# A hybrid mLSTM, convolution and expert layer on one core: TensorE sums the squares of the input piece by piece, in a kernel whose first stage is reordered by token halves

## The chip, the core and the metric

The kernel runs on one core of a Trainium2 chip. A core has five engines that run programs of their own and wait for one another by semaphores: TensorE (PE in the rows; its weight loads are shown apart as PEld), VectorE (DVE), ScalarE (ACT), GpSimd (POOL) and SyncE (SP), which here only issues DMA transfers. The metric is the device time of one execution in microseconds; lower is better. The time before is the median of three runs.

## The reference

One layer over 1024 latent tokens with a context of 256 tokens, width 1024, in float32. What matters here is how it begins:

```python
hx = _modulate(_rms_norm(x, g_pre_mix[l]), mx[0], mx[1])     # x * rsqrt(mean(x^2) + eps) * g * (1+scale) + shift
hc = _modulate(_rms_norm(ctx, g_pre_mix[l]), mc[0], mc[1])
yx, yc = _token_mixer(hx, hc, w_in[l], ...)                  # input projection, mLSTM, convolution, output projection
...
x = x + mx[5] * _rms_norm(_moe_ffn(hx, ...), g_post_ffn[l])  # 64 experts, top 8, and a shared one
```

`mx[0]` and `mx[1]` (shift and scale) are columns of `silu(c) @ w_ada + b_ada`. The norm needs, for each token, the sum of the squares of its 1024 features. After the projection there follow two scans of the mLSTM, a depthwise convolution of width 31, the output projection, the routing and the experts.

## The kernel before

`front` (L106) holds the input transposed: `X` has 8 pieces, each 128 features by 1024 tokens, loaded by eight transfers on SP's queue (L144). The stage works as follows.

- **Sums of squares** (`squares`, L147). For each piece k ScalarE writes the squares to a buffer (L151), and VectorE adds them to the sum in `vf`, the first 1024 columns of `va` (L153). So `vf` holds at the end 128 partial sums for each token.
- **Sum over partitions** (`sums`, L211). For each group of 128 tokens one matmul has the 128x128 block of `vf` as its weights and one column of ones as its moving operand (L213). VectorE scales the result (L214), and GpSimd raises it to the power of -0.5 (L215). It is done for groups 0 to 3, and then for groups 4 to 7.
- **Spread** (`spread`, L217). Four matmuls (L219) copy the four groups' factors to all 128 partitions, into half of the tile `rs`, which has 1024 columns in PSUM.
- **Scale and shift columns** (`products` and `shifts`). `products(k)` loads 1 MB of `w_ada` to a buffer `wa` and multiplies it by `silu(c)` (L183); ScalarE copies the result (L189), TensorE turns it (L192), and VectorE makes the columns `sh` and `gs` (L193, L194).
- **Modulation** (`modulate`, L222), for each piece k and each half j of 512 tokens: VectorE multiplies `X` by `gs` and `rs` (L224), ScalarE makes the rounded part `hH` (L225), VectorE the remainder `hL` (L226).
- **Projection** (`mm3`, L434). Two blocks of columns of the input weights (f = 8 and 4), each for two halves of the tokens, are accumulated over k in four PSUM tiles `pf`. Each step has three matmuls of 512 columns: `hH` by `wfH` (L436), `hL` by `wfH` (L437), `hH` by `wfL` (L438). Their weights are split in two parts by ScalarE (`wfH`, L50) and VectorE (`wfL`, L51).
- Before the first sums, six matmuls at L241 multiply pieces 3 to 5 of `X` by ones. Their results, in `rs`, are not used.

The program is written with a scheduler that keeps each engine's instructions in an order of priority; `with self.behind(...)` gives what stands in it the priority just behind the last instruction that was issued on that engine. Each engine then runs its instructions strictly in the order that came out. A float32 matmul shows in the trace as two records of TensorE, each with a weight load of its own: the four matmuls of L213 are eight records. Matmuls on the rounded parts (L436 to L438) are one record each.

What follows this stage is the rest of the projection, in which the convolution of the first blocks (`conv`, L419 on) runs on VectorE beside it, then the scans and the rest.

Of the kernel before, what the change touches and what calls it, by code (L numbers as in the profile page):

```python
# [32 lines left out]
class Layer:  # L33
# [72 lines left out]
    def front(self, cp):  # L106
# [40 lines left out]
        def squares(src, a, b):  # L147

            for k in range(8):
                sq = vf[:, NT * (1 + k % 3):][:, :b - a] if k else vf[:, a:b]  # L150
                nc.scalar.activation(sq, src[:, k], AF.Square)  # L151
                if k:
                    nc.vector.tensor_tensor(vf[:, a:b], vf[:, a:b], sq, op=OP.add)  # L153
# [10 lines left out]
        cs = small.tile([128, 8, 16, 2], F32, name="cs")  # L164
        nc.vector.tensor_copy(cs, csil.unsqueeze(2).to_broadcast([128, 8, 16, 2]))
        cs = cs.rearrange("p k r s -> p k (r s)")
        squares(X, 0, NX)
        with self.behind(mybir.EngineType.DVE):
            nc.vector.tensor_scalar(ba1[:, 8:], ba1[:, 8:], 1.0, None, op0=OP.add)
        pj, pj_ = self.pool("pj", 1, PSUM)  # L170
# [27 lines left out]
        def weights(t, pool=wf):  # L198
            if t not in wts:
                wr = wf.tile([128, 8, 128], F32, name="wfr", bufs=2)  # L200
                nc.sync.dma_start(wr, A["wf"][t])
                wH = pool.tile([128, 8, 128], F32R, name="wfH", bufs=2)
                wL = pool.tile([128, 8, 128], F32R, name="wfL", bufs=2)
                self.split(wH, wL, wr, nc.gpsimd if len(wts) > 1 else None)
                wts[t] = (wH, wL)
            return wts[t]

        ss = turned[:, :16]
        rs = pp.tile([128, NX], F32, name="rs")

        def sums(ss, a, b):  # L211
            for j in range(a, b):
                mm(ss[:, j - a:j - a + 1], vf[:, j * 128:j * 128 + 128], self.ones[:, :1], start=True, stop=True)  # L213
            nc.vector.tensor_scalar(rc[:, a:b], ss[:, :b - a], 1.0 / D, EPS, op0=OP.mult, op1=OP.add)  # L214
            nc.gpsimd.tensor_tensor(rc[:, a:b], rc[:, a:b], self.mhalf[:, a:b], op=OP.pow)  # L215

        def spread(rs, a, b):  # L217
            for j in range(a, b):
                mm(rs[:, (j - a) * 128:(j - a) * 128 + 128], rc[:, j:j + 1].to_broadcast([128, 128]), self.ident,  # L219
                   start=True, stop=True)  # L220
# [14 lines left out]

        U, Y = X[:, :4], X[:, 4:]
        first = [(f, j, pj.tile([128, 512], F32, name="pf", bufs=4)) for j in range(2) for f in (8, 4)]

        for k in range(3, 6):
            for j in range(2):  # L240
                mm(rs[:, :512], self.ones, X[:, k, 512 * j:512 * j + 512], start=True, stop=True)  # L241
        sums(ss, 0, 4)
        with self.behind():
            products(0)
        with self.behind():
            sums(ss[:, 4:], 4, 8)
        weights(8, small)
        with self.behind():
            spread(rs, 0, 4)
            shifts(0)  # L250
        with self.behind(mybir.EngineType.Activation):
            weights(4, small)
        with self.behind():
            spread(rs[:, 512:], 4, 8)
        for k in range(8):
            if k == 4:
                weights(9)
                weights(5)
            if k < 7:
                products(k + 1)  # L260
                shifts(k + 1)
            for j in range(2):
                s = slice(512 * j, 512 * j + 512)
                modulate(X[:, k, s], rs[:, s], hH[:, k, s], hL[:, k, s], k, 0)
            for f, j, ps in first:
                s = slice(512 * j, 512 * j + 512)
                self.mm3(ps, wts[f][0][:, k], wts[f][1][:, k], hH[:, k, s], hL[:, k, s], k == 0, k == 7)
        with tc.issue_after(self.wa1):
            for t, n in ((bf, "bf"), (cw, "convw"), (cv, "convv"), (ng, "normg")):
                nc.sync.dma_start(t, A[n])  # L270
# [1540 lines left out]
```

## Time and profile before

| What | Value |
|---|---|
| median of three runs | 1495.1 us (1492.36 to 1497.14) |
| the profiled execution | 1497.91 us, span 1496.1 us |
| TensorE busy | 1426.1 us, 95% of the span |
| VectorE busy | 1133.3 us, 76% |
| ScalarE busy | 753.7 us, 50% |
| GpSimd busy | 477.9 us, 32% |
| mean granted clock of TensorE | 0.986 |
| DMA | 371.64 MB, mean 248 GB/s |

The page divides the span into 40 slices of 37.4 us; TensorE is busy for 0.6 of the first one and for nearly all of the others. The stage that is changed lies in the first two slices. Times in rows are microseconds from the start of the span.

### The profile page before, as it was taken

To read this page: it belongs to the slowest core of one execution; us is meant where nothing else is said; L and a number is where in the kernel's file an instruction comes from. 1 tells how busy PE (TensorE), PEld (TensorE's weight loads), DVE (VectorE), ACT (ScalarE), POOL (GpSimd) and SP (SyncE) were. 2 spreads that over 40 slices of the span, in tenths; PEclk is the share of its full clock that TensorE was granted. 3 is DMA by queue.
4 is the path that set the end of the run, shared out by engine and by line. 5 is a ranking of instruction groups with operands and counts; after the bars stand their busy time and mean duration, and the time that the engine had idled before them with its cause. 6 is when DMAs were issued, how large, how long until landed. Compare 5 with 4: busy or idle time off the path is not lost. (4 is left out here: it accounts for less than half of the span.)

```text
span 1496.1 us, 22962 instructions
## 1 busy us (share of the span) xinstructions
PE 1426.1 (95%) x8211; PEld 1088.5 (73%) x8211; DVE 1133.3 (76%) x1942; ACT 753.7 (50%) x1241; POOL 477.9 (32%) x306
## 2 busy tenths in 40 slices
PE   6999999989999989999999999999999999999975
PEld 4688997765567755876788888888777777777764
DVE  5899979767867886744678788888777877777636
ACT  4421011245433344644566666776676767666621
POOL 1245001112213422233333333333334344455324
PEclk9999999999999999999999999999999999999998
DMA  8421051018653567997999999999999999999975
GB/s 314 176 71 43 1 189 40 19 48 287 221 187 115 193 240 275 357 294 246 306 288 327 331 322 319 333 343 339 316 342 299 321 342 310 315 352 318 337 251 209
DMA packets 94385, 371.64 MB, mean 248 GB/s; under 512 B 18269, under 2 KB 26789, under 8 KB 67770
## 3 DMA queue, kind: packets, MB, share of 16 engines
q1 hardware_dynamic: 65946, 298.48, 53.3%
q0 software_dynamic: 26032, 70.19, 19.2%
q10 hardware_dynamic: 2288, 1.45, 0.4%
q8 instruction: 66, 1.08, 0.3%
q14 instruction: 53, 0.43, 0.1%
HBM read 322.38 MB, written 62.19 MB: 257 GB/s over the span
## 5 line engine op out<-in xcount | busy, mean ns | idle before, releaser
L51 DVE TENSOR_TENSOR u<-u,u 128x1024 fp32r<-128x1024 f32 x354 | 422.0, 1220 | 124.7 <-ACT u L50 94.8
L50 ACT CAST u<-u 128x1024 fp32r<-128x1024 f32 x354 | 361.3, 1052 | 108.5 <-PE pgu L438 41.6
L1559 POOL DMA_INDIRECT acc<-yb,dst x98 | 194.4, 1983 | 351.7 <-ACT hTH L50 118.3
L436 PE MATMUL pgu<-u,xH 128*128 128x512 f32 x608 | 245.8, 404 | 0.4
L437 PE MATMUL pgu<-u,xH 128*128 128x512 f32 x608 | 238.8, 393 | 0.0
L438 PE MATMUL pgu<-u,xL 128*128 128x512 f32 x608 | 238.1, 392 | 0.0
L1439 POOL DMA_INDIRECT xg<-hxd,tok x98 | 123.6, 1261 | 194.1 <-DVE rwj L1347 68.6
L431 DVE SCALAR_TENSOR_TENSOR X<-X,cw 128x912 f32<-128x912 f32 (+14 forms) x120 | 152.0, 1291 | 1.1
L436 PEld LDWEIGHTS pgu<-u,xH 128*128 128x128 f32 x608 | 114.5, 188 | 25.5 <-ACT u L50 2.6
L438 PEld LDWEIGHTS pgu<-u,xL 128*128 128x128 f32 x608 | 114.3, 188 | 24.6
L437 PEld LDWEIGHTS pgu<-u,xH 128*128 128x128 f32 x608 | 114.5, 188 | 21.5
L436 PE MATMUL py<-u,hTH 128*128 128x512 f32 x304 | 122.1, 402 | 0.5 <-ACT hTH L50 0.5
L437 PE MATMUL py<-u,hTH 128*128 128x512 f32 x304 | 119.8, 394 | 0.0
L438 PE MATMUL py<-u,hTL 128*128 128x512 f32 x304 | 118.6, 395 | 0.0
L436 PE MATMUL pf<-hH,wfH 128*128 128x512 f32 x256 | 103.6, 408 | 0.0
L437 PE MATMUL pf<-hL,wfH 128*128 128x512 f32 x256 | 102.7, 401 | 0.7 <-DVE hL L226 0.6
L51 DVE TENSOR_TENSOR xL<-px,xH 128x512 fp32r<-128x512 f32 x152 | 97.5, 681 | 7.7 <-ACT xH L50 7.3
L438 PE MATMUL pf<-hH,wfL 128*128 128x512 f32 x256 | 102.3, 400 | 0.0
L50 ACT CAST xH<-px 128x512 fp32r<-128x512 f32 x152 | 83.9, 592 | 13.7 <-PE pgu L437 7.8
L1551 DVE COPY yb<-py 128x512 f32<-128x512 f32 x75 | 51.5, 687 | 46.3 <-PE py L438 45.8
L51 POOL TENSOR_TENSOR wfL<-wfr,wfH 128x1024 fp32r<-128x1024 f32 x14 | 48.0, 3428 | 118.2 <-ACT wfH L50 104.2
L1461 PE MATMUL px<-ident,xg 128*128 128x128 f32 x600 | 83.8, 274 | 1.1 <-DVE nl L1244 1.1
(431 smaller groups left out, 2515.6 us busy)
## 6 DMA issues: line engine op xcount, KB each, us to landing
u<-in_we_dram SPq DMA_DIRECT2D x192, 1024.0 KB
wa<-in_wa_dram SPq DMA_DIRECT2D x64, 256.0 KB
wa<-in_wa_dram SPq DMA_DIRECT2D x8, 1024.0 KB
wfr<-in_wf_dram SPq DMA_DIRECT2D x16, 512.0 KB
v<-acc SPq DMA_DIRECT2D x16, 512.0 KB
acc<-zero SPq DMA_DIRECT2D x13, 512.0 KB
u<-in_ws_dram SPq DMA_DIRECT2D x6, 1024.0 KB
X<-in_xT_dram SPq DMA_DIRECT2D x8, 512.0 KB
```

The costliest lines, as they stand in the source:

```text
L50: self.nc.scalar.copy(H, src)
L51: return (eng or self.nc.vector).tensor_tensor(L, src, H.bitcast(F32), op=OP.subtract).ins
L431: nc.vector.scalar_tensor_tensor(y[:, :, a:b], u[:, :, a + o:b + o], cw[:, i:i + 1], y[:, :, a:b], op0=OP.mult, op1=OP.add)
L436: mm(out, lH, rH, start=start, stop=False, skip_group_check=free)
L437: mm(out, lH, rL, start=False, stop=False, skip_group_check=free)
L438: mm(out, lL, rH, start=False, stop=stop, skip_group_check=free)
L1439: nc.gpsimd.indirect_dma_start(out=x[:n], out_offset=None, in_=self.hx, in_offset=bass.IndirectOffsetOnAxis(ap=self.tok[:n, c:c + 1], axis=0),
L1461: nc.tensor.transpose(pt[:, k], x[:, (4 * q + k) * 128:(4 * q + k) * 128 + 128], self.ident)
L1551: nc.vector.tensor_copy(y[:, 512:], py)
L1559: nc.gpsimd.indirect_dma_start(out=self.acc[b % NA].rearrange("r (n d) -> (r n) d", n=n), in_=y[:rows], in_offset=None, out_offset=bass.In ...
```

## The change

The additions on VectorE and the unused matmuls are gone. In place of `squares(X, 0, NX)` and of the two calls of `sums`, a new function `square_sums` squares one piece after the other into four buffers in turn, and TensorE accumulates, for each piece, eight one-column matmuls (one for each group of 128 tokens) in eight columns of PSUM. The scaling and the power are made once for all eight groups (`scales`). `rs` becomes two tiles of 512 columns, one for each half; the sums stand for a while in the second one. In the loop over k, the multiplication for the first half of piece 0 and its matmuls are issued ahead of the second half and of `products(1)`; in later steps the order is step 0, step 1, then both accumulations.

```diff
-        squares(X, 0, NX)
...
-        ss = turned[:, :16]
-        rs = pp.tile([128, NX], F32, name="rs")
+        rs = [pp.tile([128, 512], F32, name=f"rs{j}") for j in range(2)]
+
+        def square_sums(ss):
+
+            for k in range(8):
+                sq = vf[:, NT * (k % 4):][:, :NX]
+                nc.scalar.activation(sq, X[:, k], AF.Square)
+                for j in range(8):
+                    mm(ss[:, j:j + 1], sq[:, j * 128:j * 128 + 128], self.ones[:, :1], start=j + k == 0, stop=k == 7,
+                       skip_group_check=True)
+            scales(ss, 0, 8)
...
-        for k in range(3, 6):
-            for j in range(2):
-                mm(rs[:, :512], self.ones, X[:, k, 512 * j:512 * j + 512], start=True, stop=True)
-        sums(ss, 0, 4)
+        square_sums(rs[1][:, :8])
         with self.behind():
             products(0)
-        with self.behind():
-            sums(ss[:, 4:], 4, 8)
         weights(8, small)
         with self.behind():
-            spread(rs, 0, 4)
+            spread(rs[0], 0, 4)
+        with self.behind():
             shifts(0)
+            spread(rs[1], 4, 8)
         with self.behind(mybir.EngineType.Activation):
             weights(4, small)
-        with self.behind():
-            spread(rs[:, 512:], 4, 8)
         for k in range(8):
             if k == 4:
                 weights(9)
                 weights(5)
+
+            def step(j):
+                s = slice(512 * j, 512 * j + 512)
+                modulate(X[:, k, s], rs[j], hH[:, k, s], hL[:, k, s], k, 0)
+
+            def accumulate(j):
+                s = slice(512 * j, 512 * j + 512)
+                for f, i, ps in first:
+                    if i == j:
+                        self.mm3(ps, wts[f][0][:, k], wts[f][1][:, k], hH[:, k, s], hL[:, k, s], k == 0, k == 7)
+
+            if k == 0:
+                step(0)
+                accumulate(0)
             if k < 7:
-                products(k + 1)
-                shifts(k + 1)
...
+                with self.behind():
+                    products(k + 1)
+                    shifts(k + 1)
+            if k:
+                step(0)
+            step(1)
+            if k:
+                accumulate(0)
+            accumulate(1)
```

On TensorE the program began before with these rows (the line, the operation, the tile written and those read, the shape written, and how many stand in a row):

```order
L241 MATMUL rs<-X,ones 128x512 x6
L213 MATMUL pT<-ones,va 128x1 x4
L183 MATMUL a_220<-wa_239,cs 32x256 x8
L213 MATMUL pT<-ones,va 128x1 x4
L219 MATMUL rs<-ident,rc 128x128 x4
L192 MATMUL pT<-pick,a1s 128x2 x2
L219 MATMUL rs<-ident,rc 128x128 x4
L183 MATMUL a_220<-wa_281,cs 32x256 x8
L192 MATMUL pT<-pick,a1s 128x2 x2
L436 MATMUL pf<-hH,wfH 128x512 x4
L437 MATMUL pf<-hL,wfH 128x512
L438 MATMUL pf<-hH,wfL 128x512
```

With the change it begins with these (lines below the change have moved by 20: L215 is the one-column matmul of `square_sums`, L182 that of `products`, L230 the spread, L191 the turn, L456 to L458 the projection):

```order
L215 MATMUL rs_208<-ones,va 128x1 x64
L182 MATMUL a_205<-wa_287,cs 32x256 x8
L230 MATMUL rs_207<-ident,rc 128x128 x4
L191 MATMUL pT<-pick,a1s 128x2 x2
L230 MATMUL rs_208<-ident,rc 128x128 x4
L456 MATMUL pf<-hH,wfH 128x512 x2
L457 MATMUL pf<-hL,wfH 128x512
L458 MATMUL pf<-hH,wfL 128x512
L457 MATMUL pf<-hL,wfH 128x512
L458 MATMUL pf<-hH,wfL 128x512
L182 MATMUL a_205<-wa_332,cs 32x256 x8
L456 MATMUL pf<-hH,wfH 128x512 x2
```

Eight one-column matmuls have become 64, all of them ahead of `products(0)`; `products(1)` has moved from ahead of the first projection matmul to behind the first six.

On VectorE these rows stood between the making of `cs` and the first remainder `hL` before:

```order
L153 TENSOR_TENSOR va<-va 128x1024 x7
L169 TENSOR_SCALAR ba_179<-ba_179 128x8
L214 TENSOR_SCALAR rc<-pT 128x4
L51 TENSOR_TENSOR wfL<-wfr,wfH 128x1024
L214 TENSOR_SCALAR rc<-pT 128x4
L51 TENSOR_TENSOR wfL<-wfr,wfH 128x1024
L193 TENSOR_SCALAR sh<-pT,ba_179 128x2
L194 TENSOR_SCALAR gs<-pT,ba_179,gpre 128x2
L224 SCALAR_TENSOR_TENSOR X<-X,gs,rs 128x512 x2
L193 TENSOR_SCALAR sh<-pT,ba_179 128x2
L194 TENSOR_SCALAR gs<-pT,ba_179,gpre 128x2
L226 SCALAR_TENSOR_TENSOR hL<-X,sh,hH 128x512 x2
```

Now these stand there (L225 is the scaling, L192 and L193 make `sh` and `gs`, L235 and L237 are the two operations of `modulate`):

```order
L168 TENSOR_SCALAR ba_179<-ba_179 128x8
L225 TENSOR_SCALAR rc<-rs_208 128x8
L192 TENSOR_SCALAR sh<-pT,ba_179 128x2
L193 TENSOR_SCALAR gs<-pT,ba_179,gpre 128x2
L235 SCALAR_TENSOR_TENSOR X<-X,gs,rs_207 128x512
L51 TENSOR_TENSOR wfL<-wfr,wfH 128x1024 x2
L237 SCALAR_TENSOR_TENSOR hL<-X,sh,hH 128x512
L235 SCALAR_TENSOR_TENSOR X<-X,gs,rs_208 128x512
L237 SCALAR_TENSOR_TENSOR hL<-X,sh,hH 128x512
```

The seven additions are gone, and the two splits of the projection's weights (L51) have moved from ahead of the first multiplication of `X` to between it and the first `hL`. On ScalarE the copy `a1s` for `products(0)` now stands ahead of both casts to `wfH`, where it stood between them. SP's order is the same as before, and behind this stage only the interleaving of the convolution with the value projection on VectorE differs, by one instruction of the convolution.

## Rows read from the trace of the kernel before

**Rows 1.** Timeline of TensorE: start, length, line, operation, names, shape, records [idle before].

```profile
11.65 7.53 PE L241 MATMUL rs<-X,ones 128*128 128x512 f32 x12 [11.65 <-DMA X<-in_xT_dram]
```

**Rows 2.** Timeline of TensorE, later rows, same columns.

```profile
20.59 1.02 PE L213 MATMUL pT<-ones,va 128*128 128x1 f32 x8 [1.41 <-DVE ba L169]
...
22.54 1.66 PE L213 MATMUL pT<-ones,va 128*128 128x1 f32 x8
24.07 2.05 PE L219 MATMUL rs<-ident,rc 128*128 128x128 f32 x8
25.91 0.85 PE L192 MATMUL pT<-pick,a1s 128*128 128x2 f32 x4
26.63 2.05 PE L219 MATMUL rs<-ident,rc 128*128 128x128 f32 x8
28.61 1.54 PE L183 MATMUL a<-wa,cs 128*32 128x256 f32 x16
...
32.45 0.47 PE L437 MATMUL pf<-hL,wfH 128*128 128x512 f32 x1
...
34.47 1.07 PE L183 MATMUL a<-wa,cs 128*32 128x256 f32 x16
...
38.86 1.07 PE L183 MATMUL a<-wa,cs 128*32 128x256 f32 x16
```

**Rows 3.** Timeline of ScalarE, same columns.

```profile
9.22 3.88 ACT L151 ACTIVATE va<-X 128x1024 f32<-128x1024 f32 x4
...
17.64 1.06 ACT L151 ACTIVATE va<-X 128x1024 f32<-128x1024 f32 x1 [0.21 <-DMA X<-in_xT_dram]
```

**Rows 4.** Timeline of VectorE, same columns.

```profile
11.24 9.20 DVE L153 TENSOR_TENSOR va<-va 128x1024 f32<-128x1024 f32 x7 [1.39 <-ACT va L151]
...
24.32 1.22 DVE L51 TENSOR_TENSOR wfL<-wfr,wfH 128x1024 fp32r<-128x1024 f32 x1
...
26.94 0.27 DVE L194 TENSOR_SCALAR gs<-pT,ba,gpre 128x2 f32<-128x2 f32 x1
28.72 1.41 DVE L224 SCALAR_TENSOR_TENSOR X<-X,gs,rs 128x512 f32<-128x512 f32 x2 [1.51 <-PE rs L219]
...
31.62 1.41 DVE L226 SCALAR_TENSOR_TENSOR hL<-X,sh,hH 128x512 fp32r<-128x512 f32 x2
```

**Rows 5.** Timeline of GpSimd, same columns.

```profile
21.90 1.02 POOL L215 TENSOR_TENSOR rc<-rc,mhalf 128x4 f32<-128x4 f32 x1 [19.80 <-DVE rc L214]
24.48 1.94 POOL L215 TENSOR_TENSOR rc<-rc,mhalf 128x4 f32<-128x4 f32 x1 [1.57 <-DVE rc L214]
```

**Rows 6.** Timeline of TensorE in a narrow window, same columns.

```profile
23.00 1.21 PE L213 MATMUL pT<-ones,va 128*128 128x1 f32 x5
```

**Rows 7.** Timeline of TensorE's weight loads, same columns.

```profile
14.34 0.34 PEld L241 LDWEIGHTS rs<-X,ones 128*128 128x128 f32 x1 [0.52 <-issue]
15.19 0.34 PEld L241 LDWEIGHTS rs<-X,ones 128*128 128x128 f32 x1 [0.52 <-issue]
...
16.44 0.19 PEld L241 LDWEIGHTS rs<-X,ones 128*128 128x128 f32 x1 [0.24 <-issue]
16.87 0.19 PEld L241 LDWEIGHTS rs<-X,ones 128*128 128x128 f32 x1 [0.24 <-issue]
...
20.56 0.97 PEld L213 LDWEIGHTS pT<-ones,va 128*128 128x128 f32 x8 [2.21 <-issue]
```

**Rows 8.** Windows: length; busy PE, PEld, DVE, ACT, POOL; granted clock, DMA share, GB/s.

```profile
22.00:23.00 1.00, 1.00 (x16) 0.59 (x8) 0.56 (x1) 0.72 (x3) 0.92 (x1) 0.90 1.00 414
23.00:24.00 1.00, 1.00 (x6) 1.00 (x7) 0.66 (x1) 0.99 (x2) 0.00 (x0) 0.50 1.02 426
...
25.00:26.00 1.00, 1.00 (x8) 1.00 (x6) 0.55 (x1) 0.00 (x0) 1.00 (x1) 0.50 1.01 418
...
29.00:30.00 1.00, 1.00 (x16) 0.40 (x8) 1.00 (x2) 0.00 (x0) 0.00 (x0) 0.69 0.06 25
```

**Rows 9.** Waits of TensorE: total, times, longest.

```profile
PE pv L436 <- DVE gt L351: 5.3, 1, 5.3
```

More of the change, by code (lines that the diff above doesn't have):

```diff
@@ L213, in sums, with scales @@
                 mm(ss[:, j - a:j - a + 1], vf[:, j * 128:j * 128 + 128], self.ones[:, :1], start=True, stop=True)
+            scales(ss, a, b)
+        def scales(ss, a, b):
             nc.vector.tensor_scalar(rc[:, a:b], ss[:, :b - a], 1.0 / D, EPS, op0=OP.mult, op1=OP.add)
@@ L258, in front @@
                 weights(5)
-            if k < 7:
-                products(k + 1)
-                shifts(k + 1)
[L262 to L267, printed above, removed]
+            def step(j):
[9 more added lines that the diff above has]
+                accumulate(0)
+            if k < 7:
+                with self.behind():
[7 more added lines that the diff above has]
+            accumulate(1)
         with tc.issue_after(self.wa1):
```

## The prediction

> **What bounds the kernel now.** The page was read first: the span is 1496.1 us of an execution of 1497.9 us, which is 2.8 us above the median of 1495.1; the sum below is made against 1497.9 and then carried to the median. Then the timelines of the engines over the first 40 us were read side by side, since the diff touches nothing behind that, and the windows of one microsecond over the same stretch for the clock of TensorE.
>
> They show this chain. ScalarE squares the first four pieces back to back from 9.22 us, and the last one at 17.64 us, when it has landed; so the last square is there at 18.70 [rows 3]. VectorE's seven additions run beside it and end at 20.44 [rows 4]. TensorE then makes the first four sums (20.59 to 21.61), `products(0)`, and the other four sums (22.54 to 24.20), and the spreads follow [rows 2]. The power is ready 1.31 us behind the first sums (21.61 to 22.92) and 2.22 us behind the second (24.20 to 26.42) [rows 2, 5]. VectorE multiplies `X` from 28.72, the first `hL` begins at 31.62 [rows 4], and TensorE takes it up in the first L437 at 32.45; `products(2)` starts at 34.47 and `products(3)` at 38.86 [rows 2]. From there on TensorE goes in steps of 4.39 us, while VectorE needs for a step 1.41 + 1.41 + 0.45 = 3.3 us (two halves of L224, two of L226, and `sh` with `gs`, which take from the end of L192 at 26.76 to 27.21) [rows 2, 4]. TensorE is then the bound, so what comes later in the start comes later at the end.
>
> **The disputed price: one record of a one-column matmul.** The eight records at 20.59 take 1.02 us; with the last one's own 0.25 us taken off (its load begins at 20.56 and all eight loads take 0.97, so about 0.11 apart), they follow each other every 0.11 us [rows 2, 7]. The five records at 23.00 take 1.21 us; each is 0.35 us long, so they follow each other every (1.21 - 0.35) / 4 = 0.215 us [rows 6]. That is the same instruction at the two levels of the clock: the granted clock is 1.00 until it falls during the microsecond at 22, and 0.50 (1.2 GHz of 2.4) at 23 [rows 8]. What had TensorE done before it fell? It was idle for 1.41 us, then ran one-column matmuls and `products(0)` [rows 2]. And it stayed at 0.50 while TensorE was busy for the whole of each microsecond from 23, with one-column matmuls first and 128-column spreads and two-column turns behind them; it rose within the microsecond at 29, after a second spread and during the 256-column products [rows 2, 8]. At the start of the program TensorE has been idle until 11.65 and is at the lower level too: the weight loads of the unused 512-column matmuls follow each other 0.85 us apart at 14.34 and 15.19, and 0.43 apart at 16.44 and 16.87 [rows 1, 7]. Before, then, it came up while these 512-column matmuls ran, and the change takes them away.
>
> The Trainium skill, in "TensorE: Matmul & The Clock Gate", section "LDWEIGHTS (loading the stationary operand)", prices a weight load by its columns alone, whatever the clock: 128 / 1.2 = 107 ns, an estimate, 13.7 us for 128 records where the row of the lower level gives 27.5. The rows contradict it at that level (0.215 us apart), and agree at the upper one.
>
> **The change, part by part.** (1) *Added: 56 more one-column matmuls, now 64 in all.* These are 128 records, ahead of everything else in TensorE's order. Each piece brings 16 records: 16 x 0.215 = 3.4 us at the lower level and 16 x 0.11 = 1.8 us at the upper one. ScalarE delivers a piece every 0.97 us at first [rows 3]. At either level TensorE falls behind, and the pieces' arrival hides nothing but the first microseconds. I take the lower level for the whole run of 64, since in these rows the clock comes up only during other work: start 9.22 + 1.06 = 10.3, end 10.3 + 128 x 0.215 = 37.8 us, where the sums were ready at 24.20. (2) *Removed: the seven additions and the unused matmuls.* Worth at most the 18.70 to 20.59 that the first sums waited; nothing here, since TensorE is not done by then. (3) *One power for eight columns in place of two for four.* Between 1.31 and 2.22 us from the last sum [rows 2, 5]: 39.1 to 40.0. (4) *`products(0)` behind all sums.* At the lower level at least 1.54 us (the clock rose during that row), say 1.6 [rows 2]: 39.4. The power hides beside it at its lower price; at the upper it costs 0.6 more. (5) *Two tiles.* The multiplication of the first half waits for one spread only. Spread: 39.4 to 41.25 (24.07 to 25.91 before); turn 0.85: 42.1; `sh` and `gs` 0.45: 42.55; half of L224, 0.7: 43.25 [rows 2, 4]. (6) *The splits moved.* Both casts to `wfH` now stand behind the copy `a1s` of `products(0)` on ScalarE, so the splits can't run early, and on VectorE they stand ahead of the first `hL`: 2 x 1.22 = 2.45 us [rows 4], to 45.7. In the order before they lay in VectorE's waiting time. Half of L226, 0.7: the first L457 can start at 46.4, against 32.45: 14.0 us later. Had the sums taken no longer, this move alone would give back most of what the separate tiles save.
>
> (7) *First half ahead.* Before, eight matmuls lay between the first L437 and `products(2)` (2.0 us to 34.47 [rows 2]). Now there lie four matmuls for the first half, `products(1)`, six for the second half, and a turn. At 0.25 us a matmul (2.02 / 8) at the upper level, twice that at the lower, and with the clock coming up on this run of 512 columns somewhere within it: 4 x 0.45 + 1.6 + 6 x 0.25 (or 0.45) + 0.5 = 5.4 to 6.6 us. So `products(2)` starts at 51.8 to 53.0, against 34.47: 17.3 to 18.5 us later; with (3) at its upper price, up to 19.1. I take 18.
>
> (8) *Behind that.* The steps are as long as before, 4.39 us, and their transfers are issued in the same order on SP, released by the same products, so they move along. Nothing takes the delay up: the convolution on VectorE starts on results of this stage, and its backlog, for which TensorE waits 5.3 us at the value projection [rows 9], moves with it. One instruction of the convolution stands elsewhere there; up to 1 us either way.
>
> Sum: 1497.9 + 18 = 1515.9 us, and for the median 1495.1 + 18 = 1513.1.
>
> **The rivals.** *A, as above*: the lower level throughout. With its bounds (17.3 to 19.1, 1 us of the convolution and some 2 us by which the runs spread) it gives 1509 to 1518; chance 0.83. If the clock comes up only late in the first steps of the projection, it is 1 us more.
>
> *B: the clock comes up during the one-column run.* For it speaks that at the program's start it was up less than 5 us after TensorE began (at 11.65; by the spacing of the loads it was up at 16.44 [rows 1, 7]); against it, that from 23 to 29 us a busy TensorE stayed at 0.50 [rows 8]. With 4.4 us at the lower level, 20 records, and 108 at 0.11, the sums end at 10.3 + 4.4 + 11.9 = 26.6. Then `products(0)` at the upper level, 1.07 (34.47's row), spread and turn at half their rows (0.9 and 0.45), `sh` and `gs` 0.45, L224 0.7, splits 2.45, L226 0.7 [rows 2, 4]: with 0.2 for the power, 33.5 for the first L457; then 4 x 0.25 + 1.07 + 6 x 0.25 + 0.4 = 4.0: `products(2)` at 37.5, 3 us late. That is 1498, or 1497 to 1500; chance 0.10. The Trainium skill, on the same page under "What's actually happening", has a rule by which this would be the way it goes: what brings the clock up is time under sustained work and not a number of matmuls. By that rule the 64 matmuls would warm the engine themselves; the rows from 23 to 29 us, where a TensorE that never rested stayed at the lower level, don't bear it out.
>
> *C, not slower: the one-column matmuls run at 0.11 us from the first.* This needs the clock at the upper level at 10.3 us, as in a core that has just been busy. The sums then end at 10.3 + 14.1 = 24.4, about when they did, and 2.2 us ahead of B: 1496, no change. It decides when a record costs less than about 0.11; below that the change would gain. Against it stand the loads at 14.34 [rows 7]. Chance 0.04. That the change gains more than 0.3% has 0.03: it would need the sums ready by about 20 us, which even at 0.11 is not possible, so some effect that the rows don't show.
>
> **How the numbers follow.** 0.3% of 1495 is 4.5 us, about what a measurement of this kernel can tell from no change. Slower by more than that: all of A and a third of B, 0.87; within it: the rest of B and C, 0.10; faster: 0.03. The range goes down to 1500, which takes in the upper end of B and all that lies between, and up to 1519: it leaves out the lower part of B, C, and the tails of A.
>
> **What would show it.** Right: 128 records of L215 from 10.3 to about 38 us, 0.21 apart, and 0.50 in the granted clock until behind 43 us; ScalarE's squares from the fifth on waiting for TensorE to free a buffer; the first spread at about 39.5; both splits on VectorE between the first L235 and the first L237; the first L457 at about 46.5, and `products(2)` at about 52; all behind it shifted by the same 18 us. Wrong: a granted clock of 1.00 in the 64 matmuls (then B or C), one-column records closer than 0.11 us, or a stage behind 100 us in which TensorE waits less than before by more than 2 us.

## The result, and the profile after

The changed kernel takes 1517.9 us (1516.7 to 1521.4, four runs), the one before beside it 1496.1 us. The ratio is 1.0141, 95% interval 1.0117 to 1.0166: slower by 22 us. The forecast was 1513 us, slower, with a range of 1500 to 1519.

The head of the page of the changed kernel, whose execution took 1521.4 us:

```profile
span 1519.6 us, 23139 instructions
PE 1451.3 (96%) x8305; PEld 1115.3 (73%) x8311; DVE 1125.2 (74%) x1934; ACT 754.2 (50%) x1241; POOL 473.9 (31%) x305
```

TensorE is busy for 25 us more, VectorE for 8 us less: the additions went, and it did not matter. The timeline of TensorE shows where the time lies (start, length, line, operation, names, shape, records, and in brackets the idle time before and what ended it); lines stand 20 lower in the file than before, or as the change's rows gave them:

```profile
10.28 27.47 PE L215 MATMUL rs<-ones,va 128*128 128x1 f32 x128 [10.28 <-ACT va L213]
37.68 1.93 PE L182 MATMUL a<-wa,cs 128*32 128x256 f32 x16
39.74 2.08 PE L230 MATMUL rs<-ident,rc 128*128 128x128 f32 x8
41.61 0.85 PE L191 MATMUL pT<-pick,a1s 128*128 128x2 f32 x4
...
46.74 0.80 PE L457 MATMUL pf<-hL,wfH 128*128 128x512 f32 x1 [0.96 <-DVE hL L237]
47.34 0.63 PE L458 MATMUL pf<-hH,wfL 128*128 128x512 f32 x1
...
54.33 1.94 PE L182 MATMUL a<-wa,cs 128*32 128x256 f32 x16
...
57.60 0.39 PE L458 MATMUL pf<-hH,wfL 128*128 128x512 f32 x1
...
59.94 1.07 PE L182 MATMUL a<-wa,cs 128*32 128x256 f32 x16
```

The first row answers to the two rows of L213 in [rows 2]: 128 records in 27.47 us, where there were 16 in two batches; they end at 37.75 against 24.20. The first matmul on `hL` starts at 46.74 against 32.45, `products(2)` at 54.33 against 34.47, `products(3)` at 59.94 against 38.86. That is 14.3, 19.9 and 21.1 us later. The first matmuls of 512 columns are 0.63 us long and at 57.60 the same instruction is 0.39: the lower level of the clock (1.2 GHz) lasts into the second step. (The level is read from the lengths and the spacing of equal records here; the column of the granted clock says 1.00 over this whole stretch, of which more at the end of the account of the prediction.)

ScalarE, in the same columns, shows who waits for whom in the run of one-column matmuls:

```profile
9.19 3.88 ACT L213 ACTIVATE va<-X 128x1024 f32<-128x1024 f32 x4
13.94 1.06 ACT L213 ACTIVATE va<-X 128x1024 f32<-128x1024 f32 x1 [0.87 <-PE rs L215]
17.35 1.06 ACT L213 ACTIVATE va<-X 128x1024 f32<-128x1024 f32 x1 [2.36 <-PE rs L215]
...
24.18 1.06 ACT L213 ACTIVATE va<-X 128x1024 f32<-128x1024 f32 x1 [2.36 <-PE rs L215]
```

Four squares are made as in [rows 3]; each later one waits for TensorE to give a buffer back, 3.41 us apart, and the last is made at 24.18 in place of 17.64. TensorE is the one that is late.

On GpSimd and VectorE (same columns) stand the power for all eight groups and the moved splits:

```profile
38.04 1.65 POOL L226 TENSOR_TENSOR rc<-rc,mhalf 128x8 f32<-128x8 f32 x1 [35.94 <-DVE rc L225]
```

```profile
43.67 2.35 DVE L51 TENSOR_TENSOR wfL<-wfr,wfH 128x1024 fp32r<-128x1024 f32 x2
45.94 0.74 DVE L237 SCALAR_TENSOR_TENSOR hL<-X,sh,hH 128x512 fp32r<-128x512 f32 x1
```

The power ends at 39.69, and the first spread starts at 39.74; the splits lie ahead of the first `hL`, and TensorE waits for it for 0.96 us.

### The profile page after: what moved, and what is told of

It reads as the page before. It is cut to its first block, busy times and chain, and to the rows that moved or that the text cites. A ratio compares the mean times of both kernels' runs of the same rounds, so it can differ in the third digit from the quotient of the medians.

```text
span 1519.6 us, 23139 instructions
## 1 busy us (share of the span) xinstructions
PE 1451.3 (96%) x8305; PEld 1115.3 (73%) x8311; DVE 1125.2 (74%) x1934; ACT 754.2 (50%) x1241; POOL 473.9 (31%) x305
## 5 line engine op out<-in xcount | busy, mean ns | idle before, releaser
L51 DVE TENSOR_TENSOR u<-u,u 128x1024 fp32r<-128x1024 f32 x354 | 422.3, 1221 | 125.2 <-ACT u L50 95.4
L456 PE MATMUL pgu<-u,xH 128*128 128x512 f32 x608 | 246.1, 405 | 0.4
L458 PE MATMUL pgu<-u,xL 128*128 128x512 f32 x608 | 238.6, 392 | 0.0
L451 DVE SCALAR_TENSOR_TENSOR X<-X,cw 128x944 f32<-128x944 f32 (+14 forms) x120 | 152.2, 1294 | 1.1
L456 PEld LDWEIGHTS pgu<-u,xH 128*128 128x128 f32 x608 | 114.6, 188 | 25.5 <-ACT u L50 2.6
L458 PEld LDWEIGHTS pgu<-u,xL 128*128 128x128 f32 x608 | 114.6, 188 | 24.7
L456 PE MATMUL py<-u,hTH 128*128 128x512 f32 x304 | 122.3, 402 | 0.5 <-ACT hTH L50 0.5
L458 PE MATMUL py<-u,hTL 128*128 128x512 f32 x304 | 118.8, 396 | 0.0
L456 PE MATMUL pf<-hH,wfH 128*128 128x512 f32 x256 | 105.8, 416 | 0.2 <-ACT hH L236 0.2
L458 PE MATMUL pf<-hH,wfL 128*128 128x512 f32 x256 | 103.6, 405 | 0.0
L51 DVE TENSOR_TENSOR xL<-px,xH 128x512 fp32r<-128x512 f32 x152 | 97.6, 682 | 8.0 <-ACT xH L50 7.6
L51 POOL TENSOR_TENSOR wfL<-wfr,wfH 128x1024 fp32r<-128x1024 f32 x14 | 48.4, 3464 | 129.3 <-ACT wfH L50 115.3
```

The source lines that it names most:

```text
L51: return (eng or self.nc.vector).tensor_tensor(L, src, H.bitcast(F32), op=OP.subtract).ins
L451: nc.vector.scalar_tensor_tensor(y[:, :, a:b], u[:, :, a + o:b + o], cw[:, i:i + 1], y[:, :, a:b], op0=OP.mult, op1=OP.add)
L456: mm(out, lH, rH, start=start, stop=False, skip_group_check=free)
L458: mm(out, lL, rH, start=False, stop=stop, skip_group_check=free)
```

## The experiments

The theory: 64 one-column float32 matmuls are 128 records, each 0.215 us at the lower level of the clock, and these set when the stage starts. The rivals: the new order of the loop makes the loss; or the clock alone does, and not the number of records; or the buffers do. Ratios are to the kernel before on the same chip. Unless a run says otherwise, it contains the change's loop.

**The sums alone** (old loop and one tile, with the change's sums; the additions and the unused matmuls are gone here too):

```diff
-        squares(X, 0, NX)
...
-        sums(ss, 0, 4)
+        square_sums(rs[:, 512:520])
         with self.behind():
             products(0)
-        with self.behind():
-            sums(ss[:, 4:], 4, 8)
```

> The kernel before with the change's sums alone: 64 one-column matmuls and one power, in a single tile and with the old loop. Theory (64 x 2 records at the lower clock, 0.215 us apart, set the start): the sums end at 37 to 39 us and the time is 17 to 24 us above before, 1513 to 1520. Rival (the new order of the loop, with the splits and products(1) moved, makes the loss): the time is within 5 us of before.

Measured: 1516.5 us against 1498.3, ratio 1.0128 (1.0095 to 1.0161). The run of 128 records starts at 10.29 and takes 27.47 us, as in the change:

```profile
10.29 27.47 PE L216 MATMUL rs<-ones,va 128*128 128x1 f32 x128 [10.29 <-ACT va L214]
...
48.66 0.40 PE L445 MATMUL pf<-hH,wfL 128*128 128x512 f32 x1
```

One part of the change carries its loss within the interval. The last row shows a difference, though: here the projection's matmuls of 512 columns take 0.40 us from 48.66 on, in the change not before 57.60, and the convolution begins 17.4 us later than before, against 21.1 in the change. Whether the order or this one execution makes these 3.7 us, the intervals don't tell.

**The order alone** (the change with the sums, additions and unused matmuls of before; the first lines of the edit put back `squares` and take out `square_sums`):

```diff
...
-        square_sums(rs[1][:, :8])
+        for k in range(3, 6):
+            for j in range(2):
+                mm(rs[0], self.ones, X[:, k, 512 * j:512 * j + 512], start=True, stop=True)
+        sums(rs[1][:, :8], 0, 4)
         with self.behind():
             products(0)
+        with self.behind():
+            sums(rs[1][:, 4:8], 4, 8)
```

> The change without its sums: additions on VectorE, two calls of sums and the unused matmuls as before, with the two tiles and the new loop. Theory: the sums end at 24 us as before, the first matmul on hL starts between 30 and 33 us, and the time is within 4 us of before (1492 to 1500). Rival (order): 15 us or more above before.

Measured: 1499.9 us against 1498.3 in 12 runs, ratio 1.0014 (0.9998 to 1.003). That the order makes the loss is refuted. Its profiled execution was one of its fastest (1493.2 us; the 12 runs reach 1504.2), and the timeline of TensorE shows a part of the reason:

```profile
22.50 1.05 PE L212 MATMUL rs<-ones,va 128*128 128x1 f32 x8
23.41 1.14 PE L221 MATMUL rs<-ident,rc 128*128 128x128 f32 x8
...
28.12 0.39 PE L453 MATMUL pf<-hL,wfH 128*128 128x512 f32 x1
```

The second sums take 1.05 us and the spread 1.14, where [rows 2] have 1.66 and 2.05: in this execution the clock did not fall behind the unused matmuls. The first matmul on `hL` starts at 28.12, better than I expected of it. The mean granted clock of this execution, 0.989, is the highest of the twelve (0.982 to 0.988 in the others), so the others need not look like it.

**Half as many matmuls** (VectorE adds the squares of two pieces, TensorE takes the pairs):

```diff
+                if k % 2 == 0:
+                    even = sq
+                    continue
+                nc.vector.tensor_tensor(sq, sq, even, op=OP.add)
                 for j in range(8):
-                    mm(ss[:, j:j + 1], ..., start=j + k == 0, stop=k == 7,
+                    mm(ss[:, j:j + 1], ..., start=j + k == 1, stop=k == 7,
```

> The change with VectorE adding the squares of two pieces at a time, so 32 one-column matmuls in place of 64. Theory (the time is that of the records): 64 records end at 25 to 27 us, some 12 us earlier, and the time is 10 to 14 us below the change, 1504 to 1508. Rival (the loss is the lower clock of what follows and not the count of records): less than 6 us below the change.

Measured: 1506.6 us against 1498.3, ratio 1.0058 (1.0031 to 1.0085). The timeline of TensorE:

```profile
13.19 13.79 PE L219 MATMUL rs<-ones,va 128*128 128x1 f32 x64 [13.19 <-DVE va L217]
```

Half the records, half the time (13.79 against 27.47); the sums end at 27.0, 10.8 us earlier, and the excess over before falls from 21.8 to 8.3 us.

**One record for a matmul** (the squares rounded to the short format, fp32r in the rows, and kept in `hL`, which gives eight buffers; each matmul writes two equal columns; the sums lose low bits):

```diff
...
-                sq = vf[:, NT * (k % 4):][:, :NX]
+                sq = hL[:, k]
                 nc.scalar.activation(sq, X[:, k], AF.Square)
                 for j in range(8):
-                    mm(ss[:, j:j + 1], sq[:, j * 128:j * 128 + 128], self.ones[:, :1], ...
+                    mm(ss[:, 2 * j:2 * j + 2], sq[:, j * 128:j * 128 + 128], oner, ...
```

> The change with the squares rounded to the format that takes one record for a matmul (two equal columns in place of one), kept in hL: 64 matmuls, 64 records, eight buffers. The sums lose low bits. Theory (the time is records by 0.215): the sums end at 10.3 + 13.8 = 24 to 25 us, and the time is 12 to 15 us below the change, 1503 to 1506. Rival (the loss comes from the 64 instructions or from four buffers): no shorter sums with 64 instructions in the one case; in the other the squares of pieces 4 to 7 go ahead and the sums end at 37.8 all the same.

Measured: 1501.6 us against 1497.3, ratio 1.0028 (1.0012 to 1.0045). TensorE and, below it, ScalarE's last square, in the timelines:

```profile
10.27 13.81 PE L217 MATMUL rs<-oner,hL 128*128 128x2 f32 x64 [10.27 <-ACT hL L215]
```

```profile
17.53 1.06 ACT L215 ACTIVATE hL<-X 128x1024 fp32r<-128x1024 f32 x1 [0.20 <-DMA X<-in_xT_dram]
```

With 64 instructions as in the change, but 64 records, the run takes half as long; so it is records that cost, and not instructions. ScalarE now waits for the transfers alone, and the last square is there at 18.6; TensorE still works without a gap until 24.1, one record every 0.216 us. So it is not the four buffers that set the pace either. The sums end when they did before (24.20 in [rows 2]), and 4.3 us of loss remain. They arise right behind: `products(2)` starts at 38.78 in this trace, 4.3 us later than in [rows 2]; `products(1)`, which now lies between the first matmul on `hL` and it, takes 1.93 us, as at the lower level.

This run also shows who carries a late start through the program. Further on TensorE has nearly caught up, as the timelines show at its wait in the value projection (this run's row, and below it the one of before, which is the wait in [rows 9]):

```profile
156.72 0.56 PE L458 MATMUL pv<-wvH,hH 128*128 128x264 f32 x1 [8.78 <-DVE gt L373]
```

```profile
152.16 0.56 PE L436 MATMUL pv<-wvH,hH 128*128 128x264 f32 x1 [5.29 <-DVE gt L351]
```

Taking the wait from the start, it has been idle since 147.9, and in the kernel before since 146.9. So it comes 1 us late to the wait and leaves it 4.6 us late: VectorE, whose convolution began 4.9 us late, is what it waits for. (No run shortened VectorE's work there; this is read from the rows.)

**The clock up at the start** (16 unused matmuls of 512 columns ahead of the sums):

```diff
+        for n in range(16):
+            mm(rs[0], self.ones, self.ones.unsqueeze(1).to_broadcast([128, 4, 128]), start=True, stop=True)
         square_sums(rs[1][:, :8])
```

> The change with 16 unused matmuls of 512 columns (ones by ones) ahead of the sums, so that TensorE is at the upper clock when the first square arrives at about 10.3 us. Theory (at the upper clock a record costs 0.11, but the clock falls during one-column work): records 0.11 apart at first, then 0.215; the sums end at 31 to 35 us and the time is 3 to 7 us below the change, 1511 to 1515. Rival (one-column work keeps the clock up): sums at 24 to 26 us, 1497 to 1503. Rival (the clock has no part): 1517 to 1519. The order of products(1) and of the splits also moves by a few places in it.

Measured: 1518.3 us against 1498.3, ratio 1.0143 (1.011 to 1.0177). I had counted 16 records and there were 32, so they ran until 16.4 us, the sums began 6 us late and ended at 39.3 us. The time and the end of the sums miss what I expected, and the time can't be used. The windows of this run say what it was made for (length; busy PE, PEld, DVE, ACT, POOL with instructions; granted clock, DMA share, GB/s):

```profile
16.00:20.00 4.00, 4.00 (x36) 3.76 (x34) 0.00 (x0) 1.06 (x1) 0.00 (x0) 1.00 0.99 410
20.00:21.00 1.00, 1.00 (x11) 1.00 (x11) 0.00 (x0) 0.93 (x1) 0.00 (x0) 1.00 1.17 475
21.00:22.00 1.00, 1.00 (x7) 1.00 (x7) 0.00 (x0) 0.13 (x1) 0.00 (x0) 0.57 1.01 418
...
30.00:39.00 9.00, 9.00 (x44) 9.00 (x44) 0.00 (x0) 0.00 (x0) 0.00 (x0) 0.50 0.00 0
```

TensorE is busy in all of them, from 16.4 us with one-column matmuls alone. At the upper level it makes nine records in a microsecond; the clock falls within the microsecond at 21 and is at 0.50 to the end, with five records in a microsecond. This is the plain test of rival B, and refutes it for these matmuls: their run doesn't even keep a clock that is up. It also ties the spacing to the level: five records in a microsecond where the column shows 0.50.

**The same with 8 of them:**

```diff
-        for n in range(16):
+        for n in range(8):
```

> As the run with 16 unused matmuls ahead, with 8 (16 records, three to four at the lower clock and the rest at the upper: over at about 9.5 us, ahead of the first square), and the rest in the change's own order. Theory (a one-column record costs 0.11 at the upper clock, but the clock falls during one-column work, as it did 4.8 us after it began in that run): about 40 records at 0.11, the rest at 0.215; the sums end at 33 to 35 us, and the time is 3 to 5 us below the change, about 1514. Rival (the clock has no part in the loss): the sums end at 37.8.

Measured: 1513.9 us against 1497.3, ratio 1.012 (1.0092 to 1.0148): as expected. In its timeline the 16 records end at 9.82 and the run of 128 takes 23.60 us, ending at 33.97:

```profile
1.03 8.79 PE L250 MATMUL rs<-ones 128*128 128x512 f32 x16 [1.03 <-DVE third L100]
10.37 23.60 PE L215 MATMUL rs<-ones,va 128*128 128x1 f32 x128 [0.55 <-ACT va L213]
```

The clock has a part: 3.9 us off the run in the trace. By the medians it is 5.2 us off the excess (16.6 for 21.8), but the two intervals overlap, so it is the trace that shows it.

**One record, and the clock up** (both edits, with 8 unused matmuls):

> The two runs before this one in one: 64 records with the clock up at the start. Theory: each piece takes 0.9 us until the clock falls and 1.7 after; the sums end at 20 to 22 us, and the time is within 4 us of before (1494 to 1502): the loss is gone when the records are few and cheap. Rival (the new order of the loop keeps a loss of its own): 6 us or more above before.

Measured: 1499.8 us against 1497.3, ratio 1.0022 (1.0003 to 1.0041). The sums end at 21.97 us, 2.2 us earlier than before the change, and still nothing is gained. The timeline of TensorE shows that the rest of the start runs at the lower level:

```profile
10.56 11.41 PE L217 MATMUL rs<-oner,hL 128*128 128x2 f32 x64
21.91 1.93 PE L182 MATMUL a<-wa,cs 128*32 128x256 f32 x16
23.97 2.08 PE L232 MATMUL rs<-ident,rc 128*128 128x128 f32 x8
...
30.97 0.80 PE L461 MATMUL pf<-hL,wfH 128*128 128x512 f32 x1 [0.96 <-DVE hL L239]
31.56 0.63 PE L462 MATMUL pf<-hH,wfL 128*128 128x512 f32 x1
```

`products(0)` takes 1.93 us, where [rows 2] have 1.07 for such a row at the upper level, and the first projection matmuls are 0.63 us long. The first matmul on `hL` starts 1.5 us earlier than in [rows 2], but `products(2)`, with `products(1)` now ahead of it, starts at 36.65, 2.2 us later, and the excess is 2.5. One-column sums in this place leave the lower level to what follows, even where they end in time. Whether the order has a small loss of its own on top stays open; the interval of the order alone allows 4.5 us.

**The splits early** (both casts issued ahead of `products(0)`):

```diff
         square_sums(rs[1][:, :8])
+        weights(8, small)
+        weights(4, small)
         with self.behind():
             products(0)
-        weights(8, small)
...
-        with self.behind(mybir.EngineType.Activation):
-            weights(4, small)
```

> The change with both casts to wfH issued ahead of products(0), so that the splits on VectorE run while TensorE still sums, and not between the first multiplication of X and the first hL (products(1) keeps its place behind the first matmuls; the second half of the first multiplication moves up). My step 6 (the splits cost 2.45 us there): the first matmul on hL starts at 44.5 to 45.5 in place of 46.7, and the time is 1 to 3 us below the change (1515 to 1517). Rival (TensorE's clock decides from there, and what starts earlier runs longer at the lower level): the same time as the change within 1 us.

Measured: 1517.0 us against 1497.3, ratio 1.0121 (1.0098 to 1.0145); the change has 1.0141, so no difference can be told. The first matmul on `hL` starts at 47.50, later than 46.74, against my expectation. Three timelines, of GpSimd, VectorE and TensorE, show why:

```profile
38.05 2.56 POOL L226 TENSOR_TENSOR rc<-rc,mhalf 128x8 f32<-128x8 f32 x1 [35.95 <-DVE rc L225]
```

```profile
37.89 2.36 DVE L51 TENSOR_TENSOR wfL<-wfr,wfH 128x1024 fp32r<-128x1024 f32 x2
```

```profile
40.67 2.08 PE L230 MATMUL rs<-ident,rc 128*128 128x128 f32 x8 [1.04 <-POOL rc L226]
```

The splits landed beside the power, which then takes 2.56 us in place of 1.65, and TensorE waits for it before the spread, which starts 0.9 us later than in the change. So this move doesn't win back my 2.45 us for the moved splits.

**No unused matmuls** (the kernel before without L241):

```diff
-        for k in range(3, 6):
-            for j in range(2):
-                mm(rs[:, :512], self.ones, X[:, k, 512 * j:512 * j + 512], start=True, stop=True)
```

> The kernel before without its six unused matmuls. Theory (they only lift the clock): the first records of L213 are 0.215 us apart and not 0.11, the clock stays at the lower level until the projection has run for some us, and the time is 2 to 6 us above before. Rival (the start waits for transfers and VectorE, the clock is nothing there): within 1 us of before. If it costs that little, what the change loses by leaving them out is small too, and the count of records is nearly all of it.

Measured: 1499.0 us against 1497.3, ratio 1.0019 (1.0002 to 1.0035): 1.7 us by the medians and 2.8 by the ratio, at the lower end of the 2 to 6 us that I expected. The first sums run at the lower level, as the timeline shows, and the clock is up again at 30 us, much as with them:

```profile
20.45 1.84 PE L213 MATMUL pT<-ones,va 128*128 128x1 f32 x8 [20.45 <-DVE ba L169]
...
30.24 1.07 PE L183 MATMUL a<-wa,cs 128*32 128x256 f32 x16
```

With 16 records the level costs little; with 128 it doubles the run (27.5 us, where 128 at the 0.11 us of [rows 2, 7] would be some 14, an estimate). What the change loses by leaving these matmuls out is small beside the number of records.

**Order alone, with seven unused matmuls** (shown against the order alone):

```diff
...
-        for k in range(3, 6):
-            for j in range(2):
-                mm(rs[0], self.ones, X[:, k, 512 * j:512 * j + 512], start=True, stop=True)
+        for n in range(7):
+            mm(rs[0], self.ones, X[:, 3 + n // 2, 512 * (n % 2):512 * (n % 2) + 512], start=True, stop=True)
```

> The change's order and tiles with the sums of before (additions on VectorE), and with seven unused matmuls in place of six, so that TensorE rests less ahead of the sums. Theory: with a shorter rest the clock stays up more often through sums and spreads, 0.11 in place of 0.215 for each record; the first matmul on hL starts at 28 to 30, and the time is 0 to 5 us below before. Rival (the clock falls during the one-column work and the spreads all the same): no difference from before.

Measured: 1500.0 us against 1497.3, ratio 1.0008 (0.999 to 1.0025): no difference, as the rival had it. The clock fell within the microsecond at 21 in its trace, in spite of the shorter rest (0.99 us ahead of the sums, 1.41 in [rows 2]; it was 0.49 in the execution of the order alone in which the clock stayed up, and whether that is the reason is open).

**Wide sums** (two ways to make the power; both lose low bits of the sums): the squares become the moving operand, so that the means come out on all partitions. The spreads fall away, and `shifts(0)` and the second split move up.

```diff
...
+            for k in range(8):
+                nc.scalar.activation(hL[:, k], X[:, k], AF.Square)
+                for j in range(2):
+                    mm(rs[j], mean, hL[:, k, 512 * j:512 * j + 512], start=k == 0, stop=k == 7)
+            for j in range(2):
+                nc.scalar.activation(rb[j], rs[j], AF.Sqrt, bias=self.epst)
+                nc.vector.reciprocal(rb[j], rb[j])
...
```

> A way to sum on TensorE as the pieces arrive with few and wide matmuls: weights of 1/1024, the rounded squares as the moving operand of 512 columns, two matmuls of one record for each piece. The means come out on all partitions, so that spread and GpSimd's power fall away; ScalarE takes the root and VectorE the reciprocal. The sums lose low bits. Theory: TensorE keeps up with the pieces and its clock is up; the sums end at 19.5 us, the first multiplication of X starts at 24 to 26 (28.7 before), and the time is 2 to 6 us below before, 1490 to 1495. Rival (what bounds the start are the transfers and products(0), not the sums): no difference from before. If the reciprocal of 512 columns takes over 2 us, the gain is gone too.

Measured: 1503.3 us against 1497.3, ratio 1.005 (1.0031 to 1.0069). TensorE kept up: its last sum ended at 17.75 us in this trace (pieces came 0.8 us earlier). But VectorE's timeline has

```profile
19.00 6.57 DVE L221 RECIPROCAL va<-va 128x512 f32<-128x512 f32 x2 [7.20 <-ACT va L220]
...
27.97 1.41 DVE L239 SCALAR_TENSOR_TENSOR X<-X,gs,va 128x512 f32<-128x512 f32 x2
```

3.3 us for each reciprocal: the case that the expectation named. The second way, with logarithm and exponential on ScalarE and five unused matmuls around `products(0)` (shown against the first way):

```diff
-                nc.scalar.activation(rb[j], rs[j], AF.Sqrt, bias=self.epst)
-                nc.vector.reciprocal(rb[j], rb[j])
+                nc.scalar.activation(rb[j], rs[j], AF.Ln, bias=self.epst)
+                nc.scalar.activation(rb[j], rb[j], AF.Exp, scale=-0.5)
...
```

> The wide sums with the power made on ScalarE from logarithm and exponential (two table loads) in place of root and VectorE's reciprocals of 3.3 us each, and with five unused matmuls of 512 columns around products(0), so that TensorE doesn't rest. The sums lose low bits. Theory: the factors are ready at 22 to 23 us, the first multiplication of X starts at 25 to 27, the first matmul on hL at 27 to 29, and the time is 3 to 6 us below before. Rival (the transfers of weights bound the start): within 2 us of before.

Measured: 1504.3 us against 1497.3, ratio 1.0049 (1.0032 to 1.0065): a miss, and on the other side: it is slower. The first multiplication starts at 27.35, 1.4 us earlier than in [rows 4], and the first matmul on `hL` at 30.35, 2.1 us earlier than in [rows 2]; it is lost behind that. `products(2)` is already 0.4 us late (34.91), and the convolution 6.4. The windows, and below them a row of VectorE's timeline:

```profile
32.00:44.00 12.00, 11.54 (x89) 7.64 (x89) 7.95 (x15) 4.68 (x8) 1.36 (x1) 1.00 0.78 302
44.00:49.00 5.00, 3.84 (x30) 2.10 (x28) 4.06 (x4) 2.54 (x4) 2.68 (x2) 1.00 0.72 267
49.00:56.00 7.00, 6.26 (x27) 3.24 (x26) 4.42 (x7) 1.76 (x3) 0.72 (x1) 0.51 0.86 317
```

```profile
42.83 3.41 DVE L239 SCALAR_TENSOR_TENSOR X<-X,gs,va 128x512 f32<-128x512 f32 x2
```

GpSimd splits the next weights here (from 42.64 and from 47.35 us, 2.4 us each), and beside the first split VectorE's two multiplications take 3.41 us in place of 1.41. From 44 to 49 us TensorE is busy for 3.84 of 5 us, and from 49 to 56 us the clock is at 0.51. So VectorE's delay comes first in time; how much of the loss is its own and how much the clock's was not tried apart. No version in this study beats the kernel before by more than the noise.

## Why the prediction was right, step by step

- **Step 1, the price of a record and their number**: right. 128 x 0.215 = 27.5 us was forecast, 27.47 measured, from 10.28 to 37.75 (37.8 forecast). That it is records shows in the half count (13.79 us) and in one record for a matmul (13.81 us).
- **The clock stays at the lower level for the whole run**: right, and shown on its own by the run in which it was up at the start and fell. The Trainium skill's rule that I weighed there ("TensorE: Matmul & The Clock Gate", "What's actually happening": time under sustained work and not a number of matmuls) does not by itself give this: TensorE never rested for 18 us in that run and stayed at 0.50. The Trainium skill's price for a weight load by its columns alone (same page, section "LDWEIGHTS (loading the stationary operand)": 107 ns for 128 columns) agrees with the spacing of records at the upper level (0.11 us) and not at the lower one, where a record, a weight load with a matmul of one column, took 0.215 us.
- **Step 2, the additions are worth nothing**: right; VectorE is busy for 8 us less, and the stage starts later.
- **Step 3, the power**: 1.94 us from the last sum (37.75) to its end (39.69), inside 1.31 to 2.22. It was the power that released the spread, not `products(0)` as I took it, by 0.1 us. **Step 4**: 1.93 us in place of 1.6, since the clock stayed down through all of it.
- **Steps 5 and 6**: the first matmul on `hL` at 46.74, forecast 46.4. That the splits take 2.35 us there is seen in the row; that they could be had back is not shown (splits early).
- **Step 7, mis-sized**: from the first matmul on `hL` to `products(2)` I gave 5.4 to 6.6 us, with the clock coming up within it; it took 7.6 us (46.74 to 54.33). The sum priced the six matmuls and the turn ahead of `products(2)` at 2.0 to 3.2 us; at the lower level they took 3.7. The clock came up only in the next step, which took 5.6 us in place of 4.39. So `products(3)` was 21.1 us late, and not 18. The prediction had allowed 1 us for a clock that comes up late; it cost some 2.7. That is most of the miss: the excess was 21.8 us in place of 18, and the other 1 us of the 4.8 between 1513.1 and 1517.9 is the kernel before, whose median was 1496.1 this time. The result lies at the very end of rival A's 1509 to 1518.
- **Step 8, nothing takes it up**: right, and the chain is VectorE's. Its convolution starts 21.1 us later (the changed kernel's row first, then that of the kernel before, from the timelines of VectorE):

```profile
87.38 0.81 DVE L445 TENSOR_SCALAR X<-X,cw,cv 128x1024 f32<-128x1024 f32 x1
```

```profile
66.24 0.81 DVE L425 TENSOR_SCALAR X<-X,cw,cv 128x1024 f32<-128x1024 f32 x1
```

  From there to the value projection VectorE hardly rests, in either kernel. The windows, again of the changed kernel and of the one before:

```profile
84.00:174.00 90.00, 81.96 (x402) 69.34 (x400) 89.47 (x89) 20.42 (x35) 41.92 (x13) 0.97 0.20 60
```

```profile
62.00:152.00 90.00, 82.87 (x404) 69.71 (x403) 89.42 (x91) 21.18 (x37) 41.80 (x13) 0.96 0.19 60
```

  VectorE is busy for 89.4 of 90 us and TensorE for 82 to 83, so VectorE can't win a late start back. TensorE could have, up to the 5.29 us of [rows 9]: the prediction called it the bound from the first steps on, which holds only until the convolution begins. The wait there is now 6.34 us long and ends at 174.33, 22.2 us later than before; 1.3 us more come in pieces up to the end of that execution (23.5 us):

```profile
174.33 0.56 PE L456 MATMUL pv<-wvH,hH 128*128 128x264 f32 x1 [6.34 <-DVE gt L371]
```

  The median's 21.8 us is the delay of the convolution's start, within a microsecond.
- **A sign that failed**: I expected the granted clock to show 0.50 until 43 us, and named 1.00 in the 64 matmuls as the sign of B or C. The windows do show 1.00 there, and up to 58 us, though the records are 0.215 apart and neither B nor C came about. The same holds for the first microseconds of the kernel before ([rows 7] against a column that says 1.00). Where the column does show a fall, in [rows 8] and in the run with 16 unused matmuls, the spacing agrees with it. At the start of a program the spacing of equal records is the safer sign. The window of the changed kernel:

```profile
10.00:38.00 28.00, 27.72 (x132) 27.58 (x136) 0.34 (x2) 7.30 (x8) 0.00 (x0) 1.00 0.56 222
```

Side by side: when the last sum ends, how much later than at 66.24 the convolution begins (both from the profiled execution), and the excess of the median over the kernel before.

| Kernel | last sum ends, us | convolution later by, us | excess, us |
|---|---|---|---|
| order alone | 23.6 | -1.5 | 1.5 |
| no unused matmuls | 26.0 | 1.1 | 1.7 |
| one record, clock up | 22.0 | 2.8 | 2.5 |
| order alone, seven unused | 24.9 | 1.5 | 2.7 |
| one record | 24.1 | 4.9 | 4.3 |
| wide, reciprocal | 17.8 | 4.7 | 6.0 |
| wide, exponential | 19.6 | 6.4 | 7.0 |
| half count | 27.0 | 7.9 | 8.3 |
| clock up, 8 | 34.0 | 13.2 | 16.6 |
| sums alone | 37.8 | 17.4 | 18.2 |
| splits early | 37.8 | 19.7 | 19.7 |
| clock up, 16 | 39.3 | 20.8 | 19.9 |
| the change | 37.8 | 21.1 | 21.8 |

The excess follows the start of the convolution to 1.3 us in all but two, whatever made it late. The two are the order alone (3.0 us off; its profiled execution was its fastest) and the clock up with 8 unused matmuls (3.4 us, not explained here). The end of the sums alone doesn't give the excess, as the two wide runs show.

## What to carry to other kernels

Count the records that an accumulation on TensorE makes, not its columns: a float32 matmul of one column pays two full weight loads, so the sum over partitions was best made once here, after another engine had added the pieces. With the data as the wide moving operand TensorE kept up too, but the ways tried to use the result cost 6 to 7 us elsewhere. Price such a run from rows of the same instruction, at either level of the clock (here 0.215 and 0.11 us a record), and don't assume that a busy engine has the upper one: in these runs it had the lower for most of its one-column matmuls, and what came right behind them started at the lower level too. An engine with nothing to do while data arrive is free only for work that is shorter than the arrival: here the last square could be there at 18.6 us, and the sums took until 37.8. And find the engine that carries a late start on (here VectorE, through 86 us almost without a rest): what is won on another one beside it is lost again at the next wait.

## What the runs showed of the hardware that was not expected

- The clock of TensorE fell while the engine was busy without a rest: within the microsecond at 21 us, after 4.8 us of one-column matmuls alone, and it stayed at 0.50 for the remaining 18 us of them.
- GpSimd's power of eight columns took 1.65 us by itself in the change and 2.56 us beside two subtractions of 1024 columns on VectorE, with the splits early. The Trainium skill says in "GPSIMD Engine Reference", section "Specifications", that the two engines share their interfaces to SBUF, with contention where VectorE has two inputs there, as these have; these two rows agree.
- VectorE's reciprocal of 128x512 float32 elements took 3.3 us, where the two multiplications by `gs` and by the factors together take 0.7 for the same shape (L239 in the same trace).
